# Top-2 expert weights and dispatch: one queue, 16 transfers, loads of 6, 28 and 31 rows ahead of a first store of 17

## The chip, the core and the metric

The kernel runs on one core of a Trainium2 chip. The metric is device microseconds for one execution, the median over several runs. VectorE (DVE) and ScalarE (ACT) compute, SyncE (SP) and ACT issue DMA transfers, and 16 DMA engines move the data between DRAM and the core's memory of 128 partitions.

## The reference

`x` has 16 x 1024 tokens of 512 floats, `router_logits` 8 floats for each token, and k is 2. Each token is written twice, scaled by the two largest of its softmax probabilities, brought to a sum of one; the smaller comes first.

```python
probs = np.exp(router_logits - logits_max)
probs = probs / np.sum(probs, axis=-1, keepdims=True)
topk_indices = np.argsort(probs, axis=-1)[..., -k:]
topk_probs = np.take_along_axis(probs, topk_indices, axis=-1)
topk_probs = topk_probs / np.sum(topk_probs, axis=-1, keepdims=True)
x_expanded = x[:, :, np.newaxis, :].repeat(k, axis=2)
return (x_expanded * topk_probs[..., np.newaxis]).astype(np.float32)
```

So 33.6 MB of tokens and 0.5 MB of logits are read and 67.1 MB written. With the two largest logits a difference d apart, the weights are the sigmoids of -d and d.

## The kernel before

The 16,384 tokens are 128 "rows" of 128 tokens: partition p holds a run of neighbouring tokens, and a row is one token of each partition, 2 KB a partition in and 4 KB out. The rows are cut into two groups of 65 and 63 (`GROUPS`). Within a group each partition's tokens lie next to each other in DRAM, so a transfer of n rows has one piece of n x 2 KB (a load) or n x 4 KB (a store) for each of 128 partitions, eight to each of the 16 DMA engines.

`xs` holds one group of tokens (65 rows). `osp` holds 16 rows of output. Some outputs are written into `osp`, others over tokens in `xs` that have been used up (`over`, line 98).

A group goes so. First its loads are issued on SP (line 112), group 0 in pieces of 2, 4, 2, 8, 17 and 32 rows, group 1 in pieces of 16, 16 and 31 (`LOADS`, line 51). Behind the first 6 rows of group 0 the logits are loaded in two transfers (lines 116 and 117), and `top2_weights` computes all weights for both groups into `WA`: eleven small VectorE operations on pairwise maxima and minima (lines 27 to 40), then two sigmoids on ACT (lines 42 and 43).

Then `plan` (line 121) is gone through: one VectorE product (line 128) and one store (line 136) for each entry. Its rows are 2 and 14 into `osp`, 16 over `xs`, 8 and 8 into the halves of `osp`, and the rest over `xs` (9 and 8 rows in group 0, 15 in group 1, `LAST`). The store of 2 rows is issued from ACT's queue, all others from SP's, in program order. In all there are 24 transfers: 9 loads of tokens, 2 of logits, 13 stores.

What orders the work are semaphores that the framework sets: a product waits for its tokens, and for the earlier store out of the buffer that it writes; a store waits for its product; the loads of group 1 wait for the stores out of the part of `xs` that they fill. Each transfer uses one of eight DMA semaphores in turn, and one that uses a semaphore again waits for the transfer that used it before.

Of the kernel before, what the change touches and what calls it, by code (L numbers as in the profile page):

```python
# [1 line left out]

# [4 lines left out]

F32 = mybir.dt.float32
ALU = mybir.AluOpType
ACTF = mybir.ActivationFunctionType  # L10
P = 128


def top2_weights(nc, pool, logits, M, E, tag=""):

    hi, lo, n = None, None, E  # L20
    while n > 1:
        n //= 2
        if hi is None:
            a, b = logits[:, :, 0:n], logits[:, :, n : 2 * n]
            nhi = pool.tile([P, M, n], F32, tag=f"hi{n}{tag}")
            nlo = b
            nc.vector.tensor_tensor(nhi, a, b, op=ALU.max)  # L27
            nc.vector.tensor_tensor(nlo, a, b, op=ALU.min)  # L28
        else:
            a, b = hi[:, :, 0:n], hi[:, :, n : 2 * n]  # L30
            nhi = pool.tile([P, M, n], F32, tag=f"hi{n}{tag}")
            nlo = pool.tile([P, M, n], F32, tag=f"lo{n}{tag}")
            tmp = pool.tile([P, M, n], F32, tag=f"tmp{n}{tag}")
            nc.vector.tensor_tensor(tmp, lo[:, :, 0:n], lo[:, :, n : 2 * n], op=ALU.max)  # L34
            nc.vector.tensor_tensor(nlo, a, b, op=ALU.min)  # L35
            nc.vector.tensor_tensor(nlo, nlo, tmp, op=ALU.max)  # L36
            nc.vector.tensor_tensor(nhi, a, b, op=ALU.max)  # L37
        hi, lo = nhi, nlo
    dlt = pool.tile([P, M], F32, tag=f"dlt{tag}")
    nc.vector.tensor_tensor(dlt, hi[:, :, 0], lo[:, :, 0], op=ALU.subtract)  # L40
    WA = pool.tile([P, M, 2], F32, tag=f"WA{tag}")
    nc.scalar.activation(WA[:, :, 0], dlt, ACTF.Sigmoid, scale=-1.0)  # L42
    nc.scalar.activation(WA[:, :, 1], dlt, ACTF.Sigmoid, scale=1.0)  # L43
    return WA

GROUPS = [65, 63]

LOADS = [[2, 4, 2, 8, 17, 32], [16, 16, 31]]


LAST = [[(48, 9), (57, 8)], [(48, 15)]]


@with_exitstack
def kernel(
    ctx: ExitStack,
    tc: tile.TileContext,  # L60
    x: bass.AP,
    router_logits: bass.AP,
    k: bass.AP,
    out: bass.AP,
):
    nc = tc.nc
    B, S, D = x.shape
    E = router_logits.shape[-1]
    N = B * S
    assert int(k) == 2 and E == 8 and N == P * sum(GROUPS)  # L70
    M = N // P

    L = 16
    x_v, o_v, rl_v = [], [], []
    t0 = 0
    for n in GROUPS:
        t1 = t0 + P * n
        x_v.append(
            x.rearrange("b s d -> (b s) d")[t0:t1].rearrange("(p m) d -> p m d", p=P)
        )  # L80
        o_v.append(
            out.rearrange("b s k d -> (b s) k d")[t0:t1].rearrange(
                "(p m) k d -> p m k d", p=P
            )
        )
        rl_v.append(
            router_logits.rearrange("b s e -> (b s) e")[t0:t1].rearrange(
                "(p m) e -> p m e", p=P
            )
        )  # L90
        t0 = t1

    wpool = ctx.enter_context(tc.tile_pool(name="wpool", bufs=1))
    logits = wpool.tile([P, M, E], F32)
    xs = wpool.tile([P, max(GROUPS), D], F32)
    osp = wpool.tile([P, L, 2, D], F32)

    def over(r, n, G):

        a = 2 * r - G
        return xs[:, a : a + 2 * n, :].rearrange("p (r k) d -> p r k d", k=2)

    h = L // 2
    e = 2
    m0 = 0
    for g, G in enumerate(GROUPS):
        r = 0  # L110
        for n in LOADS[g]:
            nc.sync.dma_start(xs[:, r : r + n, :], x_v[g][:, r : r + n, :])  # L112
            r += n
            if g == 0 and r == 6:

                nc.sync.dma_start(logits[:, :G], rl_v[0])  # L116
                nc.sync.dma_start(logits[:, G:], rl_v[1])
                WA = top2_weights(nc, wpool, logits, M, E)
        assert r == G
        begin = [(0, e, osp[:, :e]), (e, L - e, osp[:, e:])]  # L120
        plan = begin + [
            (L, L, over(L, L, 2 * L)),
            (2 * L, h, osp[:, :h]),
            (2 * L + h, h, osp[:, h:]),
        ]
        plan += [(r, n, over(r, n, G)) for r, n in LAST[g]]
        for r, n, og in plan:
            nc.vector.tensor_tensor(  # L128
                og,
                xs[:, r : r + n, :].unsqueeze(2).to_broadcast([P, n, 2, D]),  # L130
                WA[:, m0 + r : m0 + r + n, :].unsqueeze(3).to_broadcast([P, n, 2, D]),
                op=ALU.mult,
            )

            queue = nc.scalar if n == e else nc.sync
            queue.dma_start(o_v[g][:, r : r + n], og)
        m0 += G


# [1 line left out]
_INS = ['x', 'router_logits', 'k']  # L141
_OUTS = [((16, 1024, 2, 512), 'float32')]

_NUMBERS = {'k': 2}


# [26 lines left out]
```

## Time and profile before

| | |
|---|---|
| median of the runs | 240.22 us (240.09 to 240.84) |
| span of the profiled execution | 239.1 us |
| VectorE busy | 142.1 us (59%), 24 instructions |
| ScalarE busy | 1.8 us (1%), 3 instructions |
| DMA packets | 3456, of which 24 x 128 carry data and 24 x 16 write semaphores |
| moved | 101.19 MB, mean 423 GB/s over the span |
| share of the 16 DMA engines | SP's queue (q1) 96.5%, ACT's queue (q10) 2.1% |

The profiled execution has its own time, the span, from its first to its last instruction; the runs are other executions and include what lies around it. Times in the profile's rows are microseconds from the start of the span. L128 is line 128 of the kernel; SPq and ACTq are the engines' queues that issue DMA. A DMA packet counts for the stretch in which it starts, with the whole of its time, so shares of a short stretch can pass 100%.

### The profile page before, as it was taken

The page shows a single profiled execution, that of the slowest core. Times are in us where ns is not written, and L with a number is a line of the kernel's source. Part 1 is how long each engine was busy: PE and PEld are TensorE (multiplying, and loading weights), DVE is VectorE, ACT ScalarE, POOL GpSimd, SP SyncE. Part 2 cuts the span into 40 slices and gives each one's busy share as a digit, 9 for nine tenths or more (in the row PEclk, how much of TensorE's full clock was granted, in tenths as well). Part 3 has the DMA queues.
Part 4 walks back from the last instruction along what each step waited for, and adds up shares of the span by engine and source line. Part 5 has one row for each costly group of instructions (what it writes and reads, how often), then busy time and mean ns, then how long its engine had stood idle before and what let it go on. Part 6 is the DMA issues. An engine that isn't in the chain of part 4 may idle for free.

```text
span 239.1 us, 118 instructions
## 1 busy us (share of the span) xinstructions
DVE 142.1 (59%) x24; ACT 1.8 (1%) x3; POOL 0.2 (0%) x4
## 2 busy tenths in 40 slices
DVE  0589999900299699900000699999006999990000
ACT  2000000000000000000000000000000000000000
POOL 0000000000000000000000000000000000000000
DMA  7999989899999999999999999899899898999894
GB/s 254 440 463 426 441 388 526 329 460 460 417 438 406 400 422 438 438 481 396 433 438 438 438 511 396 384 502 394 384 460 515 362 493 367 428 433 486 380 483 175
DMA packets 3456, 101.19 MB, mean 423 GB/s; under 512 B 384, under 2 KB 512, under 8 KB 896
## 3 DMA queue, kind: packets, MB, share of 16 engines
q1 hardware_dynamic: 3168, 99.09, 96.5%
q10 hardware_dynamic: 288, 2.10, 2.1%
HBM read 34.08 MB, written 67.11 MB: 423 GB/s over the span
## 4 chain that ended last, share of the span: by engine, by line
DMA 52%; DVE 33%; issue 4%; SPq 1%; ACT 0%; DVEq 0%
DMA out_dram<-xs 24%; DVE xs L128 18%; DVE osp L128 13%; DMA out_dram<-osp 13%; DMA xs<-in_x_dram 13%; DMA logits<-in_router_logits_dram 3%; SPq L112 0%; DVE nhi L27 0%; DVE logits L28 0%; DVE nlo L36 0%; DVE nhi L37 0%; DVE nlo L35 0%; DVE tmp L34 0%; SPq L116 0%; ACT WA L42 0%
## 5 line engine op out<-in xcount | busy, mean ns | idle before, releaser
L128 DVE TENSOR_TENSOR osp<-xs,WA 128x8192 f32<-128x8192 f32 (+2 forms) x8 | 69.2, 8688 | 62.3 <-DMA xs<-in_x_dram 31.2
L128 DVE TENSOR_TENSOR xs<-xs,WA 128x16384 f32<-128x16384 f32 (+3 forms) x5 | 69.1, 13811 | 2.2 <-DMA out_dram<-xs 2.0
L27 DVE TENSOR_TENSOR nhi<-logits 128x512 f32<-128x512 f32 x1 | 0.7, 691 | 8.5 <-DMA logits<-in_router_logits_dram 8.5
L42 ACT ACT_TABLE_LOAD x1 | 1.3, 1283 | 0.7 <-PEq L154 0.7
L28 DVE TENSOR_TENSOR logits<-logits 128x512 f32<-128x512 f32 x1 | 0.7, 691 | 0.0
L35 DVE TENSOR_TENSOR nlo<-nhi 128x256 f32<-128x256 f32 (+1 forms) x2 | 0.7, 351 | 0.0
L37 DVE TENSOR_TENSOR nhi<-nhi 128x256 f32<-128x256 f32 (+1 forms) x2 | 0.7, 351 | 0.0
L36 DVE TENSOR_TENSOR nlo<-nlo,tmp 128x256 f32<-128x256 f32 (+1 forms) x2 | 0.7, 350 | 0.0
L34 DVE TENSOR_TENSOR tmp<-logits 128x256 f32<-128x256 f32 x1 | 0.4, 417 | 0.0
L42 ACT ACTIVATE WA<-dlt 128x128 f32<-128x128 f32 x1 | 0.3, 315 | 10.4 <-DVE dlt L40 10.4
L40 DVE TENSOR_TENSOR dlt<-nhi,nlo 128x128 f32<-128x128 f32 x1 | 0.3, 291 | 0.0
L43 ACT ACTIVATE WA<-dlt 128x128 f32<-128x128 f32 x1 | 0.3, 298 | 0.0
L34 DVE TENSOR_TENSOR tmp<-nlo 128x128 f32<-128x128 f32 x1 | 0.3, 283 | 0.0
L154 POOL MEMSET const-bfloat16-1.0<- 128x1 bf16 x1 | 0.1, 101 | 0.0
L154 POOL MEMSET const-uint8-127<- 128x1 uint8 x1 | 0.1, 101 | 0.0
L154 POOL MEMSET const-float32-0.0<- 128x1 f32 x1 | 0.1, 98 | 0.2 <-issue 0.2
L154 POOL MEMSET const-float32-1.0<- 128x1 f32 x1 | 0.1, 98 | 0.0
## 6 DMA issues: line engine op xcount, KB each, us to landing
out_dram<-osp SPq DMA_DIRECT2D x4, 4096.0 KB, 20.7
out_dram<-osp SPq DMA_DIRECT2D x2, 7168.0 KB, 32.4
xs<-in_x_dram SPq DMA_DIRECT2D x2, 4096.0 KB, 30.4
xs<-in_x_dram SPq DMA_DIRECT2D x1, 7936.0 KB, 40.9
out_dram<-xs SPq DMA_DIRECT2D x1, 7680.0 KB, 23.1
out_dram<-xs SPq DMA_DIRECT2D x1, 4608.0 KB, 20.4
xs<-in_x_dram SPq DMA_DIRECT2D x1, 4352.0 KB, 22.8
out_dram<-xs SPq DMA_DIRECT2D x1, 4096.0 KB, 21.4
```

The costliest lines, as they stand in the source:

```text
L27: nc.vector.tensor_tensor(nhi, a, b, op=ALU.max)
L28: nc.vector.tensor_tensor(nlo, a, b, op=ALU.min)
L34: nc.vector.tensor_tensor(tmp, lo[:, :, 0:n], lo[:, :, n : 2 * n], op=ALU.max)
L35: nc.vector.tensor_tensor(nlo, a, b, op=ALU.min)
L36: nc.vector.tensor_tensor(nlo, nlo, tmp, op=ALU.max)
L37: nc.vector.tensor_tensor(nhi, a, b, op=ALU.max)
L40: nc.vector.tensor_tensor(dlt, hi[:, :, 0], lo[:, :, 0], op=ALU.subtract)
L42: nc.scalar.activation(WA[:, :, 0], dlt, ACTF.Sigmoid, scale=-1.0)
L43: nc.scalar.activation(WA[:, :, 1], dlt, ACTF.Sigmoid, scale=1.0)
L128: nc.vector.tensor_tensor(og, xs[:, r : r + n, :].unsqueeze(2).to_broadcast([P, n, 2, D]), WA[:, m0 + r : m0 + r + n, :].unsqueeze(3).to_b ...
L154: nc = _bacc.Bacc("TRN2", target_bir_lowering=False, num_devices=1)
```

## The change

- Group 0 is loaded in 6, 28 and 31 rows instead of six pieces. The logits still stand behind the first 6 rows.
- Each group has four stores: 17, 16, 16, 16 rows in group 0, and 16, 16, 16, 15 in group 1 (`STORES`). The first and third come out of `osp`, the second and fourth over `xs`. All are issued from SP, so ACT's queue issues none. In all there are 16 transfers: 6 loads of tokens, 2 of logits, 8 stores.
- `osp` has 18 rows instead of 16. The logits and the scratch of `top2_weights` lie in its last three rows (15 to 17) until the weights are done; they had buffers of their own.
- The last two rows of group 0's first store, and the last four of each third store, are computed by ACT: two `Copy` activations of 512 elements for each row, with the weight as scale. VectorE computes the other 15 and 12. Everything else remains with VectorE.
- The store of 17 rows has 69,632 B a partition, and is built as 128 x 2 pieces of 34,816 B.

The diff, cut to its core:

```diff
-LOADS = [[2, 4, 2, 8, 17, 32], [16, 16, 31]]
-LAST = [[(48, 9), (57, 8)], [(48, 15)]]
+LOADS = [[6, 28, 31], [16, 16, 31]]
+STORES = [
+    [
+        (17, ("osp", 0), 2, "SP"),
+        (16, ("x", 1), 0, "SP"),
+        (16, ("osp", 0), 4, "SP"),
+        (16, ("x", 33), 0, "SP"),
+    ],
+    [
+        (16, ("osp", 0), 0, "SP"),
+        (16, ("x", 0), 0, "SP"),
+        (16, ("osp", 0), 4, "SP"),
+        (15, ("x", 33), 0, "SP"),
+    ],
+]
+OSP = 18
...
+    osp = pool.tile([P, OSP, 2, D], F32)
+    WA = pool.tile([P, M, 2], F32)
+    logits = osp[:, OSP - 1].rearrange("p k d -> p (k d)").rearrange("p (m e) -> p m e", e=E)
+    scratch = osp[:, OSP - 3 : OSP - 1].rearrange("p r k d -> p (r k d)")
...
+        for n, (home, a), by_act, queue in STORES[g]:
+            if home == "x":
+                og = xs[:, a : a + 2 * n, :].rearrange("p (r k) d -> p r k d", k=2)
+            else:
+                og = osp[:, a : a + n]
+            v = n - by_act
+            w = WA[:, m0 + r : m0 + r + n, :]
+            if v:
+                nc.vector.tensor_tensor(
+                    og[:, :v],
+                    xs[:, r : r + v, :].unsqueeze(2).to_broadcast([P, v, 2, D]),
+                    w[:, :v].unsqueeze(3).to_broadcast([P, v, 2, D]),
+                    op=ALU.mult,
+                )
+            for i in range(v, n):
+                for c in range(2):
+                    nc.scalar.activation(
+                        og[:, i, c], xs[:, r + i, :], ACTF.Copy, scale=w[:, i, c : c + 1]
+                    )
+            {"SP": nc.sync, "ACT": nc.scalar}[queue].dma_start(o_v[g][:, r : r + n], og)
+            r += n
```

`top2_weights` does the same eleven VectorE operations and two sigmoids on the same shapes; it takes its intermediate buffers out of `scratch`.

More of the change, by code (lines that the diff above doesn't have):

```diff
@@ L11 @@
 P = 128
-def top2_weights(nc, pool, logits, M, E, tag=""):
-    hi, lo, n = None, None, E
+E = 8
+D = 512
+GROUPS = [65, 63]
+M = sum(GROUPS)
+LOADS = [[6, 28, 31], [16, 16, 31]]
[13 more added lines that the diff above has]
+]
@@ L21, in top2_weights, with cut @@
+OSP = 18
+def top2_weights(nc, scratch, logits, WA):
+    used = [0]
+    def cut(n):
+        a = scratch[:, used[0] : used[0] + M * n].rearrange("p (m n) -> p m n", n=n)
+        used[0] += M * n
+        return a
+    a, b = logits[:, :, 0:4], logits[:, :, 4:8]
+    hi = cut(4)
+    lo = b
+    nc.vector.tensor_tensor(hi, a, b, op=ALU.max)
+    nc.vector.tensor_tensor(lo, a, b, op=ALU.min)
+    n = 4
     while n > 1:
         n //= 2
[L23 to L37, printed above, removed]
@@ L38, in top2_weights @@
-        hi, lo = nhi, nlo
[L39 to L49, printed above, removed]
-LOADS = [[2, 4, 2, 8, 17, 32], [16, 16, 31]]
-LAST = [[(48, 9), (57, 8)], [(48, 15)]]
+        a, b = hi[:, :, 0:n], hi[:, :, n : 2 * n]
@@ new lines, in top2_weights @@
+        nhi, nlo, tmp = cut(n), cut(n), cut(n)
+        nc.vector.tensor_tensor(tmp, lo[:, :, 0:n], lo[:, :, n : 2 * n], op=ALU.max)
+        nc.vector.tensor_tensor(nlo, a, b, op=ALU.min)
+        nc.vector.tensor_tensor(nlo, nlo, tmp, op=ALU.max)
+        nc.vector.tensor_tensor(nhi, a, b, op=ALU.max)
+        hi, lo = nhi, nlo
+    dlt = cut(1)
+    nc.vector.tensor_tensor(dlt, hi, lo, op=ALU.subtract)
+    nc.scalar.activation(WA[:, :, 0], dlt[:, :, 0], ACTF.Sigmoid, scale=-1.0)
+    nc.scalar.activation(WA[:, :, 1], dlt[:, :, 0], ACTF.Sigmoid, scale=1.0)
@@ L66 @@
     nc = tc.nc
[L67 to L73, printed above, removed]
+    N = x.shape[0] * x.shape[1]
+    assert int(k) == 2 and router_logits.shape[-1] == E and x.shape[2] == D
+    assert N == P * M
+    xf = x.rearrange("b s d -> (b s) d")
+    of = out.rearrange("b s k d -> (b s) k d")
+    rf = router_logits.rearrange("b s e -> (b s) e")
     x_v, o_v, rl_v = [], [], []
@@ L77, with load_logits @@
         t1 = t0 + P * n
[L78 to L90, printed above, removed]
-        t0 = t1
[L93 to L107, printed above, removed]
+        x_v.append(xf[t0:t1].rearrange("(p m) d -> p m d", p=P))
+        o_v.append(of[t0:t1].rearrange("(p m) k d -> p m k d", p=P))
+        rl_v.append(rf[t0:t1].rearrange("(p m) e -> p m e", p=P))
+        t0 = t1
+    pool = ctx.enter_context(tc.tile_pool(name="pool", bufs=1))
+    xs = pool.tile([P, max(GROUPS), D], F32)
+    osp = pool.tile([P, OSP, 2, D], F32)
+    WA = pool.tile([P, M, 2], F32)
+    logits = osp[:, OSP - 1].rearrange("p k d -> p (k d)").rearrange("p (m e) -> p m e", e=E)
+    scratch = osp[:, OSP - 3 : OSP - 1].rearrange("p r k d -> p (r k d)")
+    def load_logits():
+        nc.sync.dma_start(logits[:, : GROUPS[0]], rl_v[0])
+        nc.sync.dma_start(logits[:, GROUPS[0] :], rl_v[1])
     m0 = 0
@@ L112 @@
             nc.sync.dma_start(xs[:, r : r + n, :], x_v[g][:, r : r + n, :])
+            if g == 0 and r < 6 <= r + n:
+                load_logits()
+                top2_weights(nc, scratch, logits, WA)
             r += n
[L114 to L118, printed above, removed]
         assert r == G
[L120 to L136, printed above, removed]
+        r = 0
+        for n, (home, a), by_act, queue in STORES[g]:
[19 more added lines that the diff above has]
+            r += n
+        assert r == G
         m0 += G
```

## The prediction

> **What bounds the kernel now.** I read the page first: span, busy engines, share of the DMA engines, queues, and the time to landing of the last store.
>
> ```profile
> span 239.1 us, 118 instructions
> DVE 142.1 (59%) x24; ACT 1.8 (1%) x3; POOL 0.2 (0%) x4
> ...
> DMA  7999989899999999999999999899899898999894
> DMA packets 3456, 101.19 MB, mean 423 GB/s; under 512 B 384, under 2 KB 512, under 8 KB 896
> q1 hardware_dynamic: 3168, 99.09, 96.5%
> q10 hardware_dynamic: 288, 2.10, 2.1%
> ...
> out_dram<-xs SPq DMA_DIRECT2D x1, 7680.0 KB, 23.1
> ```
>
> VectorE works 59% of the span, the 16 DMA engines 96.5 + 2.1 = 98.6% of it, in every slice but the first and the last. Then I asked by stretch where the missing 1.4% lies, and the timeline for the first issue and the last.
>
> ```profile
> 0.00:1.74 1.74, 0.00 (x0) 1.01 (x1) 0.20 (x4) 1.00 0.00 0
> 164.00:236.00 72.00, 37.41 (x4) 0.00 (x0) 0.00 (x0) 1.00 1.00 432
> ...
> 0.73 0.86 SPq L112 DMA_DIRECT2D xs<-in_x_dram  x2
> 215.19 0.33 SPq L136 DMA_DIRECT2D out_dram<-xs  x1
> ```
>
> In a row by stretch the last two columns are DMA share and GB/s. Nothing moves before 1.74; the share is 1.00 while the last four stores drain, though VectorE works only 37.41 of those 72 us. The last store lands 23.1 us after its issue at 215.19, at 238.3. So the time is 1.74 us of start, then the length of an unbroken DMA queue, then some 0.8 us of ending. Idle VectorE time costs nothing, and an edit counts only if it changes what a DMA engine spends on a packet, or opens a hole in the queue. The profiled execution spans 239.1 us and the median of the runs is 240.2; I carry differences from one to the other unchanged.
>
> **What a packet costs.** The DMA view of a narrow stretch counts packets, MB and share, and share times length times 16, divided by packets, is the time of one packet. Here are the answers for 47.2 to 62 us, 63.9 to 80, and 84 to 91.5.
>
> ```profile
> q1 hardware_dynamic: 112, 6.42, 100.1%
> ...
> q1 hardware_dynamic: 98, 6.36, 91.1%
> ...
> q1 hardware_dynamic: 97, 3.18, 98.1%
> ```
>
> The first holds 14-row store packets (57,344 B): 14.8 x 1.001 x 16 / 112 = 2.116 us. The second holds 97 packets of 65,536 B and a semaphore write: 16.1 x 0.911 x 16 / 97 = 2.419 us. The third holds 32,768 B packets: 7.5 x 0.981 x 16 / 97 = 1.214 us. Two of the last make one of the second plus 0.008 us, so a packet costs about 0.008 us of its own and the rest is bytes.
>
> **Fewer, larger transfers.** Before there are 24 transfers of 128 packets, 24 x 8 = 192 packets on each engine. After there are 16, and the store of 17 rows, 69,632 B a partition, is built as two pieces each, so 17 x 8 = 136 packets. The bytes are the same. Saved: 56 x 0.008 = 0.45 us, on the path, because the queue is the path. The first load goes from 2 + 4 rows to 6 in one; its bytes ahead of the logits are the same, and 8 packets fewer is 0.06 us, counted already.
>
> The Trainium skill says otherwise: "DMA: Bandwidth & Descriptors", section "Anatomy of one DMA", fits 2.0 us of fixed cost to each transfer beside its bytes. By it, an estimate, eight transfers fewer would take off 16 us; the share of 1.00 at 432 GB/s in the row from 164 to 236 disagrees, for no engine idles between transfers there.
>
> **The store beside the loads.** ACT's queue (q10) carries 2 rows in each group beside SP's loads. Its issue, then the stretches from 15.3 to 18.78 and from 18.78 to 20.7:
>
> ```profile
> 15.32 0.38 ACTq L136 DMA_DIRECT2D out_dram<-osp  x1
> ...
> q1 hardware_dynamic: 38, 1.32, 88.3%
> ...
> q1 hardware_dynamic: 23, 0.80, 96.9%
> q10 hardware_dynamic: 20, 0.16, 20.2%
> ```
>
> Beside q10 the loads' 34,816 B packets take 1.92 x 0.969 x 16 / 23 = 1.293 us. Scaled from the 1.214 us row by bytes they would take 0.008 + 1.206 x 34,816 / 32,768 = 1.289. So taking the store away from the loads frees under 0.005 us for each packet, nothing I can count.
>
> **From load to store.** Two stretches hold exactly the last packet of each engine ahead of a group's first large store, 43.2 to 43.9 us (16 packets of 65,536 B) and 160.4 to 161.5 (16 of 63,488 B).
>
> ```profile
> q1 hardware_dynamic: 16, 1.05, 433.8%
> ...
> q1 hardware_dynamic: 16, 1.02, 224.1%
> ```
>
> They took 0.7 x 4.338 = 3.04 us and 1.1 x 2.241 = 2.47 us, where 2.419 and 2.343 are usual: 0.62 us lost in group 0, 0.12 in group 1. Group 1's change keeps its 31-row load and a large store behind it, so 0.12 stays. In group 0 the load of 32 rows becomes one of 31, like group 1's, so the loss may stay at 0.62 or fall to 0.12, and with a hole at the seam to zero: 0 to -0.6 us. The nearest row in size is group 1's, but I can't say size is the cause; I take -0.25.
>
> **The slowest engine.** The 16 semaphore writes of the last store, in 236.5 to 237.2, 237.2 to 237.8 and 237.8 to 238.2:
>
> ```profile
> q1 hardware_dynamic: 14, 0.00, 1.1%
> ...
> q1 hardware_dynamic: 1, 0.00, 0.1%
> q1 hardware_dynamic: 1, 0.00, 0.1%
> ```
>
> One engine of 16 finishes over 0.6 us behind 14 of the others, and it sets the end. That is an accident of this execution as far as the trace tells. Another chain of larger packets may have a better or worse one, between -0.7 and +0.3 us; I take -0.2.
>
> **The seam of group 0, where the change takes its risk.** Before, the first large store is ready long ahead of the queue's need. After, its 15 VectorE rows need the load of 28 rows. The rows, the first of them the DMA packets from 8.0 to 8.53 us:
>
> ```profile
> DMA packets 52, 0.21 MB, mean 402 GB/s; under 512 B 0, under 2 KB 0, under 8 KB 52
> ...
> 8.53 0.69 DVE L27 TENSOR_TENSOR nhi<-logits 128x512 f32<-128x512 f32 x1 [8.53 <-DMA logits<-in_router_logits_dram]
> ...
> L128 DVE TENSOR_TENSOR xs<-xs,WA 128x16384 f32<-128x16384 f32 x2 | 34.4, 17224 | 0.1
> L128 DVE TENSOR_TENSOR osp<-xs,WA 128x14336 f32<-128x14336 f32 x2 | 30.2, 15084 | 0.0
> L128 DVE TENSOR_TENSOR xs<-xs,WA 128x15360 f32<-128x15360 f32 x1 | 16.2, 16158 | 0.0
> ...
> L128 DVE TENSOR_TENSOR osp<-xs,WA 128x8192 f32<-128x8192 f32 x4 | 34.6, 8688 | 30.6 <-DMA out_dram<-osp 30.6
> L42 ACT ACTIVATE WA<-dlt 128x128 f32<-128x128 f32 x1 | 0.3, 315 | 10.4 <-DVE dlt L40 10.4
> ```
>
> VectorE sees the logits at 8.53, after it 8.47. The 28 rows follow: 8 x 2.116 = 16.93, seen at 25.40. The product of 15 rows takes 16.16: 41.56. SP then issues the store. The load of 31 rows takes 8 x 2.343 = 18.74 more and would be seen at 44.14. By the rows at 43.2 and 43.9 plus 3.04 us the engines of before went on to the store between 46.2 and 46.9, spread over 0.7 us; and a landing is seen some 0.5 us after the last engine's data (no packet under 2 KB, so none of the logits' and no semaphore write of theirs, after 8.0). So after the change they run dry from 42.9 to 43.6.
>
> How long from issue to first packet? The first load's row says 0.73 to 1.74, 1.0 us, into empty engines. ACT's says 15.32 to 18.78, 3.5 us, into engines full with another queue's packets. By the first the store starts at 42.6, ahead of the dry point by 0.3 to 1.0 us. By the second it starts at 45.0, and 1.4 to 2.1 us are lost. I take the first, because at the seam no other queue holds packets in front; allowing for the last engines to be served, +0.1 us. The Trainium skill, same page, section "Queues, rings and completion order", has each DMA engine take turns between queues by whole packets; by that, 3.5 us would be mostly a wait for a turn, which one queue alone doesn't have. No run here shows it yet.
>
> **The rest of the chain has room.** ACT's two rows are four activations of 512 elements; at most 4 x 0.315 = 1.26 us each, 5.0 us, beside VectorE's 16.16. Group 0's second store: VectorE 41.56 + 17.22 = 58.8, while the queue is busy with 17 rows to about 43.3 + 8 x 2 x 1.289 = 63.9. Third: the wait for that store's landing ends near 64.5, 12 rows take 12.95 (between the rows of 8,192 and 14,336 elements) to 77.5, ACT's four rows at most 8 x 1.26 = 10.1 us beside it; the queue needs it at 63.9 + 19.35 = 83.3. Fourth: 94.7 against 102.6. Group 1: loads run from about 122 to 160; VectorE has the first 16 rows near 132.5 and the product at 149.7 against 160. Third: 180.3 + 12.95 = 193.3 against 198.8. The least of these margins is 5 us, so a product given up to ACT or a shared buffer costs nothing there; if the cover failed, only what exceeds 5 us would show. SP's queue is in order, and no load stands behind a store that comes late: the loads of group 1 are issued after 94.7 and needed at 122. The two logits loads and the scratch in `osp` add no wait, since rows 15 and 16 of the first store are written by ACT behind its own sigmoids.
>
> **Sum.** -0.45 - 0.25 - 0.2 + 0.1 = -0.8 us: 238.3 us of span, 239.4 us as a median.
>
> **Rivals.** A measurement of this kernel can tell about 0.3%, 0.72 us: faster is below 239.5, slower above 240.94.
>
> *Only the packets count.* The switch from load to store costs 0.6 again and a straggler of the same size appears: -0.45 + 0.1, 239.9 us, no change that can be told. For it: two of my four terms are accidents of one execution. Chance 0.30.
>
> *The hole at the seam.* The store of 17 rows starts as ACT's row had it, 3.5 us from issue. It decides once issue to first packet passes about 1.6 us, or VectorE is late by 0.6 us. At 3.5 us the hole is 1.75 on average: -0.45 - 0.2 + 1.75 = +1.1, 241.3 us. Against it: the row of the first load, and that issue still comes a microsecond before the dry point. Chance 0.20, of which 0.03 with a small hole ends within 0.3%.
>
> *A fixed cost for each transfer after all.* By a mechanism that the share of 1.00 would have to hide, eight transfers would give 16 us, 224 us. Chance 0.01; the page named above is its only source.
>
> *The change doesn't do what it says.* The two pieces per partition of the 17-row store fall unevenly on the engines: if some engine had twice 20.6 us, 20 us more, 260 us. Nothing in the trace has such a shape; all that it has run evenly. Chance 0.02.
>
> The forecast itself has 0.47. Faster: 0.47 + 0.01 = 0.48. Within 0.3%: 0.30 + 0.03 = 0.33. Slower: 0.17 + 0.02 = 0.19. The forecast's own range is 238.6 (switch and straggler both gone) to 239.5. The range for 8 in 10 reaches up through the first rival and most of the hole, 238.6 to 241.2.
>
> **What would show it.** Right: the DMA share near 1.00 from 2 to 236 with q10 gone, 136 data packets an engine, the first packet of the 17-row store about 1 us after SP's issue near 41.6. Wrong: a stretch near 43 us with a low share; VectorE's product of 15 rows starting after 25.4 or lasting over 16.2 us; a last load packet again near 3.0 us; the last semaphore write no earlier than 237.8.

## The result, and the profile after

The changed kernel takes 242.22 us (241.44 to 242.77, 6 runs) against 240.16 (240.02 to 240.84, 6 runs) for the kernel before: 1.008 times, interval 1.0068 to 1.0092. It is slower, by 2.06 us. The forecast was 239.4, range 238.6 to 241.2.

The page of the changed kernel, the lines that answer to those of before:

```profile
span 240.4 us, 125 instructions
DVE 131.0 (54%) x19; ACT 14.4 (6%) x23; POOL 0.2 (0%) x4
...
DMA  7997998899998989898969999998989999999894
DMA packets 2432, 101.19 MB, mean 421 GB/s; under 512 B 256, under 2 KB 384, under 8 KB 512
q1 hardware_dynamic: 2432, 101.19, 98.3%
```

The same bytes go in 2432 packets instead of 3456, and the DMA engines are busy for 98.3% of a longer span, against 98.6% before. So no large hole stands in the queue. Packets take longer, and the engines end further apart.

The queue turns three times: from group 0's loads to its stores, from these to group 1's loads, and from those to group 1's stores. I call these the first, second and third turn, and what a packet takes there beyond its usual time the loss. The next fence has the DMA view of the changed kernel for stretches that hold just the 16 packets around each turn. The columns are packets, MB and share. In order: 40.53 to 41.03 us (last load packets before the first turn), 119.1 to 119.85 (last store packets before the second), 122.4 to 123.2 (first load packets behind it, with 16 semaphore writes of 0.01 us), 158.2 to 160.35 (last load packets before the third).

```profile
q1 hardware_dynamic: 16, 1.02, 468.6%
...
q1 hardware_dynamic: 16, 1.05, 422.2%
...
q1 hardware_dynamic: 32, 0.52, 178.3%
...
q1 hardware_dynamic: 16, 1.02, 144.7%
```

Worked out as in the prediction, a packet at the first turn takes 0.5 x 4.686 = 2.34 us, the usual time. At the second it takes 0.75 x 4.222 = 3.17 where 2.42 is usual, behind it 0.8 x 1.783 - 0.01 = 1.42 where 1.21 is, and at the third 2.15 x 1.447 = 3.11 where 2.34 is. So each engine loses nothing at the first turn, 0.75 + 0.20 at the second and 0.77 at the third. Before, the first cost 0.62 and the third 0.12. The second cost nothing there: its last store packets, from 121.1 to 122.1 us in the kernel before, took 1.0 x 1.213 = 1.21 us, the usual time for 32,768 B.

```profile
q1 hardware_dynamic: 16, 0.52, 121.3%
```

The four stores between the first two turns also run a little long. From 82.81 to 100.45 us, 128 packets of 65,536 B and 16 semaphore writes:

```profile
q1 hardware_dynamic: 144, 8.39, 110.2%
```

That is 17.64 x 1.102 x 16 / 128 = 2.430 us a packet against 2.419, 0.08 us a transfer. By the packet records of the trace the four stores of group 0 lose 0.23 together.

Last, the semaphore writes of the last store, from 237.3 to 238.6 and from 238.6 to 239.4:

```profile
q1 hardware_dynamic: 15, 0.00, 0.6%
...
q1 hardware_dynamic: 1, 0.00, 0.1%
```

The engines end scattered over two microseconds, one far behind.

**Which execution the profile of before showed.** With every run's span beside its time, the two differ by about 1.8 us in both kernels: 242.22 and 240.4 after, 240.16 and 238.4 before. The profiled execution of before had a span of 239.1, so it was the run of 240.84, the slowest of the first three, and not a typical one. Typical executions lie 2.0 us apart in span, not 1.3.

### The profile page after: what moved, and what is told of

The parts are those of the page before. It is cut to its first block, busy times and chain, and to the rows that moved or that the text cites. A ratio compares the mean times of both kernels' runs of the same rounds, so it can differ in the third digit from the quotient of the medians.

```text
span 240.4 us, 125 instructions
## 1 busy us (share of the span) xinstructions
DVE 131.0 (54%) x19; ACT 14.4 (6%) x23; POOL 0.2 (0%) x4
## 2 busy tenths in 40 slices
DMA packets 2432, 101.19 MB, mean 421 GB/s; under 512 B 256, under 2 KB 384, under 8 KB 512
## 3 DMA queue, kind: packets, MB, share of 16 engines
q1 hardware_dynamic: 2432, 101.19, 98.3%
## 4 chain that ended last, share of the span: by engine, by line
DMA 48%; DVE 39%; SPq 1%; issue 0%; DVEq 0%
DMA xs<-in_x_dram 26%; DVE osp L126 25%; DMA out_dram<-osp 23%; DVE xs L126 14%; SPq L105 0%; SPq L104 0%; SPq L111 0%; SPq L137 0%; DVEq L126 0%
## 5 line engine op out<-in xcount | busy, mean ns | idle before, releaser
L126 DVE TENSOR_TENSOR osp<-xs,WA 128x12288 f32<-128x12288 f32 (+2 forms) x4 | 59.3, 14825 | 72.6 <-DMA xs<-in_x_dram 52.4
L126 DVE TENSOR_TENSOR xs<-xs,WA 128x16384 f32<-128x16384 f32 (+1 forms) x4 | 67.8, 16958 | 0.3
L134 ACT ACTIVATE osp<-xs,WA 128x512 f32<-128x512 f32 x20 | 12.6, 708 | 162.8 <-DMA out_dram<-osp 150.3
L52 DVE TENSOR_TENSOR osp<-osp 128x512 f32<-128x512 f32 x1 | 0.7, 693 | 8.2 <-DMA osp<-in_router_logits_dram 8.2
L66 ACT ACTIVATE WA<-osp 128x128 f32<-128x128 f32 x1 | 0.3, 315 | 10.2 <-DVE osp L65 10.2
L53 DVE TENSOR_TENSOR osp<-osp 128x512 f32<-128x512 f32 x1 | 0.7, 692 | 0.0
L60 DVE TENSOR_TENSOR osp<-osp 128x256 f32<-128x256 f32 (+1 forms) x2 | 0.7, 352 | 0.0
L62 DVE TENSOR_TENSOR osp<-osp 128x256 f32<-128x256 f32 (+1 forms) x2 | 0.7, 352 | 0.0
L61 DVE TENSOR_TENSOR osp<-osp 128x256 f32<-128x256 f32 (+1 forms) x2 | 0.7, 352 | 0.0
L59 DVE TENSOR_TENSOR osp<-osp 128x256 f32<-128x256 f32 (+1 forms) x2 | 0.7, 351 | 0.0
L67 ACT ACTIVATE WA<-osp 128x128 f32<-128x128 f32 x1 | 0.3, 297 | 0.0
## 6 DMA issues: line engine op xcount, KB each, us to landing
xs<-in_x_dram SPq DMA_DIRECT2D x2, 7936.0 KB, 40.6
```

The lines of the kernel that those rows point to most:

```text
L52: nc.vector.tensor_tensor(hi, a, b, op=ALU.max)
L53: nc.vector.tensor_tensor(lo, a, b, op=ALU.min)
L66: nc.scalar.activation(WA[:, :, 0], dlt[:, :, 0], ACTF.Sigmoid, scale=-1.0)
L67: nc.scalar.activation(WA[:, :, 1], dlt[:, :, 0], ACTF.Sigmoid, scale=1.0)
L126: nc.vector.tensor_tensor(og[:, :v], xs[:, r : r + v, :].unsqueeze(2).to_broadcast([P, v, 2, D]), w[:, :v].unsqueeze(3).to_broadcast([P, v ...
L134: nc.scalar.activation(og[:, i, c], xs[:, r + i, :], ACTF.Copy, scale=w[:, i, c : c + 1])
```

## The experiments

Four theories came up, one after the other. Theory 1: a packet before a turn takes longer when one of 65,536 B stands beside the turn. Theory 2: a turn always costs, by how the engines stand to each other. Theory 3, after the first four runs: a first turn that is covered, with its store issued early, costs something once and makes the later ones free, and the change's seam (its first turn) misses that. Theory 4, its rival: where the buffers lie. Below, the dry point is the moment when the engines run out of group 0's load packets, 42.9 us for the first of them in the changed kernel, and the lead of a store is how long before that it is issued.

**Smaller packets at the turns.** Twice in the changed kernel:

```diff
 a1: -(16, ("x", 33), 0, "SP")     +(8, ("x", 33), 0, "SP"), (8, ("x", 49), 0, "SP")
     -(16, ("osp", 0), 0, "SP")    +(8, ("osp", 0), 0, "SP"), (8, ("osp", 8), 0, "SP")
 a2: -(16, ("x", 33), 0, "SP")     +(1, ("x", 33), 0, "SP"), (15, ("x", 35), 0, "SP")
     -(16, ("osp", 0), 0, "SP")    +(14, ("osp", 0), 0, "SP"), (2, ("osp", 14), 0, "SP")
```

> The changed kernel with the last store of group 0 cut into 8 + 8 rows and the first store of group 1 cut into 8 + 8, so packets of 32,768 B stand on the store side of the second and third turn of the queue. Theory 1 (the last packet of each engine before a turn is stretched when a packet of 65,536 B stands on either side): the stretch before the second turn falls from 0.75 us to under 0.1, that of the first packets behind it from 0.21 to under 0.1, and the one before the third turn from 0.77 to under 0.15; two transfers more cost 0.13 us; span 240.4 - 1.5 = 238.9, time about 240.7 us. Theory 2 (the stretch comes with a turn whatever the sizes, and its size is set by how the engines stand to each other): all three stay within 0.3 us of what they were, span 240.4, time 242.2 us. Both: the time outside the span stays at 1.8 us, since ACT issues no transfer here either.

> The changed kernel with the last store of group 0 cut into 1 + 15 rows (packets of 61,440 B before the second turn) and the first store of group 1 into 14 + 2 (packets of 57,344 B behind the third, as in the kernel before). Theory 1a (it takes a packet of exactly 65,536 B): both stretches fall to 0.15 us or less, span about 239.1. Theory 1b (it grows with the size): second turn about 0.7 us, third about 0.7 us, span 240.4. Theory 2: no change beyond 0.3 us at each turn.

Measured: 242.18 us (1.0072, 1.0053 to 1.009) and 241.97 (1.0075, 1.0057 to 1.0094). The DMA view of a1 before the second turn, 120.3 to 121.3 us, and before the third, 158.3 to 160.05:

```profile
q1 hardware_dynamic: 16, 0.52, 201.4%
...
q1 hardware_dynamic: 16, 1.02, 169.5%
```

Packets of 32,768 B take 2.01 us where 1.21 is usual, a loss of 0.80 as with packets twice the size. At the third turn 2.97, a loss of 0.62. In a2 the losses are 0.59 and 0.95. Theory 1 falls: no loss went below 0.15 us. Theory 2 had these numbers about right, but it is too simple: a1's second turn moves the very rows that the kernel before moves there, where it loses nothing.

**ACT's queue, in both directions.** The last store of the changed kernel from ACT's queue, and the kernel before without ACT's queue:

```diff
 a3: -(15, ("x", 33), 0, "SP")                        +(15, ("x", 33), 0, "ACT")
 b1: -queue = nc.scalar if n == e else nc.sync        +queue = nc.sync
```

> The changed kernel with the very last store issued from ACT's queue instead of SP's. Inside the span theories 1 and 2 both expect 240.4 within 0.3 us: the turns stand as they were, and the last store drains beside the one before it. For the 0.76 us by which the time outside the span grew (1.06 before, 1.82 after): if it hangs on ACT's queue carrying no transfer, it falls back to about 1.1 us here and the time is about 241.5; if it hangs on the 20 activations or anything else in the change, it stays at 1.8 and the time is 242.2.

> The kernel before with its two stores of 2 rows issued from SP's queue like the others, so that no store runs beside loads. The prediction's reading: no difference inside the span beyond 0.2 us. Theory 2 in the form that stores beside the loads keep the engines out of step: the stretch before the third turn rises from 0.12 to 0.6 us or more. Theory 1: the packet behind both turns is one of 8,192 B, the packet before them 65,536 B in the first and 63,488 B in the third; first turn 0.3 to 0.6 us, third under 0.15. Outside the span: 1.8 us if it hangs on ACT's queue, 1.1 if not.

Measured: a3 241.71 us (1.0059, 1.0041 to 1.0078), b1 240.26 (1.0006, 0.9995 to 1.0016). In a3 the second turn loses 0.63 and 0.21 behind it, the third 1.03. The 1.8 us outside the span is there in all four, so the question about it rested on the untypical execution of before. That no store runs beside loads costs and brings nothing by itself: b1's first turn, from 40.65 to 41.3 us, takes 3.12 where 2.42 is usual, a loss of 0.70, its third, from 158.15 to 158.9, 2.42 where 2.34 is, and its engines end together, all 16 semaphore writes between 236.6 and 237.5:

```profile
q1 hardware_dynamic: 16, 1.05, 480.0%
...
q1 hardware_dynamic: 16, 1.02, 322.1%
...
q1 hardware_dynamic: 16, 0.00, 1.0%
```

**The seam covered, the buffers moved, the two pieces gone.**

```diff
 c1: -LOADS = [[6, 28, 31], [16, 16, 31]]     +LOADS = [[6, 11, 17, 31], [16, 16, 31]]
 c2: +pad = pool.tile([P, 1024], F32)         (ahead of xs)
     +nc.gpsimd.memset(pad[:, 0:1], 0.0)
 c3: before: logits = wpool.tile(...) moved behind osp
 c4: -(17, ("osp", 0), 2, "SP")               +(16, ("osp", 0), 2, "SP"), (1, ("osp", 16), 0, "SP")
```

> The changed kernel with group 0 loaded in 6, 11, 17 and 31 rows, so that the first store of 17 rows is ready some 12 us ahead of the first turn instead of 1.5. Theory 3 (the engines' places to each other: the stretch at a first turn that is covered puts the engines into an order in which later turns are free, and the seam of the change, run nearly dry, skips that): 0.6 us stretch at the first turn, then under 0.15 at the second and third, and no stretch in the stores between; span about 238.5. Theory 4 (where the buffers lie): about 0.6 us more at the first turn, second and third stay near 0.75 (with 0.25 behind the second) and 0.75, span about 241.

> The changed kernel with a buffer of 4,096 B a partition put ahead of xs, which puts xs where it lay in the kernel before (the logits' buffer stood there). Theory 4: second and third turn fall under 0.15 us, stores between 43 and 123 us lose their 0.2 us of stretch, span about 238.7. Theory 3: nothing changes, span 240.2 to 240.7.

> The kernel before with its logits buffer allocated behind osp, so that xs starts at the bottom as in the changed kernel. Theory 4: second and third turn rise to 0.6 us or more, time 241.5 us or more. Theory 3: no change, 240.2 us.

> The changed kernel with the store of 17 rows made as 16 and 1, so that no partition's run is cut into two pieces of 34,816 B; the seam is 1.1 us earlier. If the two pieces throw the engines out of order, the stores between 43 and 123 us lose their stretch, and second and third turn fall to 0.15 us or less: span about 238.6. Theories 3 and 4: second and third turn stay at 0.6 us or more each, span 240.2 to 240.8.

Measured: c1 240.39 us (1.0003, 0.9993 to 1.0012), c2 241.88 (1.0071, 1.005 to 1.0091), c3 240.23 (0.9994, 0.9981 to 1.0006), c4 241.19 (1.0032, 1.0018 to 1.0047). Theory 4 falls with c2 and c3 as the cause of the loss. c2's second turn loses 0.52, with 0.48 behind it, and its third 0.29; its span of 239.9 us lies under what theory 3 had, so whether the place of the buffers moves part of the loss stays open. c3's turns lose 0.38, 0 and 0.22. c1 gives back all that the change lost. Its DMA view, 40.6 to 41.1 us (before the first turn), 120 to 120.55 (second), 158.1 to 159 (third), and the last semaphore writes, 236.5 to 237.5:

```profile
q1 hardware_dynamic: 16, 1.02, 690.7%
...
q1 hardware_dynamic: 16, 1.05, 439.6%
...
q1 hardware_dynamic: 16, 1.02, 263.3%
...
q1 hardware_dynamic: 16, 0.00, 0.9%
```

A packet at the first turn takes 3.45 us where 2.34 is usual and loses 1.11, more than the 0.6 expected. The second is free (2.418), the third nearly (2.37), and the engines end together. c4 came out in between, as no theory had it: its store is issued a microsecond earlier than in the changed kernel, and its turns lose 0.32, 0.27 and 0.71. Its ten runs lie spread from 240.14 to 241.90 us, from c1's time nearly to the changed kernel's. It removed the stretch of the stores between, but two pieces are not the cause, since c1 has them and no stretch either.

c4's trace also shows the first two turns engine by engine, since each packet begins within some 5 ns of the end of the one before it on its engine, and so each engine's packets can be followed. The ten engines that lost 0.29 us or more at the first turn lost at most 0.17 at the second, and the four that lost nothing at the first lost 0.57 to 0.98 there. The third turn is not freed in this way: it cost every engine 0.31 us or more, also those that had paid.

**The lead alone.** c1 also changed the pieces of the loads. d1, e3 and d2 leave them as they are and move only the issue of the first store, by the rows that ACT takes:

```diff
 d1: -(17, ("osp", 0), 2, "SP")     +(17, ("osp", 0), 6, "SP")
 e3: -(17, ("osp", 0), 2, "SP")     +(17, ("osp", 0), 4, "SP")
 d2: -(17, ("osp", 0), 2, "SP")     +(17, ("osp", 0), 0, "SP")
```

> The changed kernel, loads as they are, with six instead of two of the first store's 17 rows given to ACT, so that VectorE's product has 11 rows and the store is issued near 36.9 us, some 6 us ahead of the dry point instead of 1.5. If the early issue is what counts (theory 3), and not that the loads come in more pieces: 0.4 to 1.1 us of stretch at the first turn, under 0.15 at the second and third, no stretch in the stores between, time about 240.4 us. If the pieces of the loads did it: no change, first turn 0, second 0.75 and more, third about 0.75, time 242.2.

> The changed kernel with four rows of the first store on ACT: VectorE's product 14.0 us, store issued near 39.3, 3.6 us ahead of the dry point. Leads so far: 1.5 us, turns of 0, 1.0 and 0.77; 2.6 us (with 16 and 1 rows), 0.32, 0.27 and 0.71; 5.8 us, 1.11, 0.03 and 0.05. If the lead has to exceed what one packet of the last load takes, 2.34 us, plus a start of about 1 us: first turn near 1.1, second and third under 0.15, time 240.4. If it takes two packets, 4.7 us and a start: in between as at 2.6 us, time 241.2.

> The changed kernel with all 17 rows of the first store on VectorE: product 18.3 us, store issued near 43.5, so that the engines stand empty for 1.0 to 1.7 us. Theory 3: first turn without stretch, second and third stretched as in the changed kernel, about 1.7 us together; the hole comes on top, span 241.5 to 242.2, time 243.3 to 244.0. A rival, that a near miss at the seam does the harm and a clean hole resets the engines: second and third under 0.15, time about 242.0 us.

Measured: d1 240.49 us (1.0012, 1.0003 to 1.0021), e3 240.41 (1.001, 1.0000 to 1.0019), d2 242.43 (1.0094, 1.0077 to 1.0111). The issue in e3's timeline, and its last load packets before the first turn, from 40.55 to 41.2 us:

```profile
39.43 0.40 SPq L137 DMA_DIRECT2D out_dram<-osp  x1
...
q1 hardware_dynamic: 16, 1.02, 520.6%
```

They take 0.65 x 5.206 = 3.38 us, a loss of 1.04, and the second and third turn lose 0.00 and 0.04. d1, issued at 37.12, loses 1.11, 0.00 and 0.05. The lines for e3's second turn (120.0 to 120.57 us) and its third (158.15 to 158.75):

```profile
q1 hardware_dynamic: 16, 1.05, 424.2%
...
q1 hardware_dynamic: 16, 1.02, 397.7%
```

Two microseconds of lead, got from two rows more on ACT, are all that lies between the changed kernel's 242.22 us and 240.41. c1 moves the lead by the loads and leaves ACT's rows alone, d1 and e3 do the opposite, and all three come out the same.

In d2 the store comes too late: its issue, the DMA packets from 43.3 to 44.35 us, then from 44.35 to 44.51, and the last packets before the second turn (120.75 to 120.95) and the third (159.7 to 160.1):

```profile
43.44 0.40 SPq L137 DMA_DIRECT2D out_dram<-osp  x1
...
q1 hardware_dynamic: 1, 0.00, 0.1%
...
q1 hardware_dynamic: 16, 0.56, 808.6%
...
q1 hardware_dynamic: 16, 1.05, 1601.6%
...
q1 hardware_dynamic: 16, 1.02, 787.8%
```

Nothing but a semaphore write for a microsecond, then all engines start within 0.16 us, 0.9 us after the issue. Second and third turn lose 0.79 and 0.81. So a hole doesn't reset anything, and theory 3 stands. I had expected 243.3 or more. The hole of about 1.3 us cost only 0.2 beside the changed kernel: d2's engines, which start together, also end together (all between 238.7 and 239.6), and in its trace no engine lags behind the rest.

**What the first turn costs.** c1 with the last load packets smaller, and with a store on ACT's queue beside the loads as before:

```diff
 d3: +LOADS = [[6, 11, 17, 27, 4], [16, 16, 31]]
 d4: +LOADS = [[6, 11, 17, 16, 15], [16, 16, 31]]
 e1: c1 with (17, ("osp", 0), 2, "SP") -> (2, ("osp", 0), 0, "ACT"), (15, ("osp", 2), 2, "SP")
 e2: e1 with (16, ("osp", 0), 0, "SP") -> (2, ("osp", 0), 0, "ACT"), (14, ("osp", 2), 0, "SP")
```

> The kernel with the covered seam (group 0 in 6, 11, 17 and 31 rows: first turn 1.11 us, time 240.39) with its 31 rows cut into 27 and 4, so that the last packets before the first turn have 8,192 B. If the stretch at a covered first turn grows with the packet before it: under 0.5 us, second and third stay under 0.15, time about 239.8. If it is a fixed price of that turn: 0.6 to 1.1 us, time 240.4.

> The kernel with the covered seam with its 31 rows cut into 16 and 15, last packets of 30,720 B. By size: first turn 0.4 to 0.7 us, time about 240.1. Fixed price: 0.6 to 1.1 us, time 240.4. Theory 3 for both: second and third turn under 0.15 us.

> The kernel with the covered seam (loads of 6, 11, 17, 31), with group 0's first store as in the kernel before: 2 rows issued from ACT beside the loads, then 15 from SP (two of them computed by ACT; no two-piece store, 16 other transfers, 136 packets an engine). In the kernels whose ACT queue carries a store beside group 0's loads the first turn cost 0.62 and 0.38 us, in those without 0.70 to 1.11. If the store beside the loads is what makes the turn cheaper: first turn 0.4 to 0.6 us, second and third under 0.25, time 239.7 us, a little under the kernel before. If not: first turn 0.7 to 1.1, time 240.3.

> The same, with 2 rows from ACT's queue ahead of 14 in group 1 too. If a store beside the loads always softens the turn behind it: third turn 0 to 0.1 us, time 239.7. If it unsettles an order that was there (third turn 0.12 and 0.22 us in the kernels before with it, 0.03 to 0.08 in those without): third turn 0.1 to 0.25, time 239.9.

Measured: d3 240.48 us (1.0013, 1.0002 to 1.0025), d4 240.35 (1.0006, 0.9991 to 1.0022), e1 240.15 (0.9995, 0.9986 to 1.0003), e2 240.23 (1.0000, 0.9991 to 1.0009). Size isn't it: d3's load of 4 rows loses 1.09 us in all, with packets an eighth as large, and d4's last load 0.82. d3's third turn loses 0.27, where I had expected less than 0.15; its trace is of its slowest run, 241.00 us. With ACT's store e1 loses 0.60 and e2 0.49 at the turn, but their loads beside that store lose 0.15 and 0.28 more, so the two together come to about 0.75. e1 is the best of the changed design, and ties with the kernel before; neither e1 nor e2 reached the 239.7 us that a cheaper first turn was to bring.

One table has the kernels that differ in lead; the losses are microseconds for each engine, worked out from each trace as above. The lead is the issue of group 0's first large store ahead of 42.9 us, where the changed kernel's first engine runs dry; for the kernel before, ahead of 46.2 us, where its own engines get to the store. The others side with their leads: a1, a2, a3 and c2, as late as the changed kernel, lose nothing at the first turn and 1.3 to 1.9 behind it, and b1, c3, d3, d4, e1 and e2, all early, lose 0.38 to 1.09 at the first and at most 0.27 at a later one.

| kernel | lead, us | first turn | second, and behind it | third | time, us |
|---|---|---|---|---|---|
| d2 | -0.5 | 0 and a hole | 0.79, 0.16 | 0.81 | 242.43 |
| changed | 1.5 | 0 | 0.75, 0.20 | 0.77 | 242.22 |
| c4 | 2.6 | 0.32 | 0.27, 0.01 | 0.71 | 241.19 |
| e3 | 3.5 | 1.04 | 0, 0 | 0.04 | 240.41 |
| d1 | 5.8 | 1.11 | 0, 0 | 0.05 | 240.49 |
| c1 | 11.7 | 1.11 | 0, 0 | 0.03 | 240.39 |
| before | 16 | 0.62 | 0, 0 | 0.12 | 240.16 |

## Why the prediction was wrong

**The packets: right.** 19 x 128 packets and semaphore writes are left, a full packet takes 2.42 us in group 1's stores as before, and 56 x 0.008 = 0.45 us of the queue is gone. The 2.0 us for each transfer, which the prediction took from the Trainium skill ("DMA: Bandwidth & Descriptors", "Anatomy of one DMA"), is measured there for a transfer issued from GpSimd. It is no price in this queue: c1, with 17 transfers, takes 1.0003 times as long as the kernel before with 24.

**The seam: right in its times, wrong in what it decides.** The timeline of the changed kernel:

```profile
25.19 16.16 DVE L126 TENSOR_TENSOR osp<-xs,WA 128x15360 f32<-128x15360 f32 x1 [13.06 <-DMA xs<-in_x_dram]
41.44 0.40 SPq L137 DMA_DIRECT2D out_dram<-osp  x1
41.45 17.23 DVE L126 TENSOR_TENSOR xs<-xs,WA 128x16384 f32<-128x16384 f32 x1
58.71 0.35 SPq L137 DMA_DIRECT2D out_dram<-xs  x1
64.50 12.96 DVE L126 TENSOR_TENSOR osp<-xs,WA 128x12288 f32<-128x12288 f32 x1 [5.82 <-DMA out_dram<-osp]
```

25.19, 41.44, 58.71 and 64.50 stand against 25.40, 41.56, 58.8 and 64.5 forecast. The first store packets start at 42.94 us, where the first engine runs dry, and the hole over all engines is below 0.1 us, as taken. Issue to first packet is 0.9 us in d2's empty engines, near the row that I took and not ACT's 3.5. The rival with the hole, which held most of my chance of slower, didn't happen. (Its price of +1.1 left out the -0.6 at the first turn that I had myself given to a hole; with it the sum is +0.5.) What I missed is that a seam just short of a hole takes the loss from the first turn and puts more of it on the next two.

**From load to store: the step that failed.** I counted 0.62 us at the first turn as something local that could stay, shrink or vanish, and took -0.25. It vanished, -0.62. But I wrote of the third turn that its 0.12 "stays", because its load kept its size, and I had no term for the second at all, since nothing showed there. The third went to 0.77, the second to 0.75 + 0.20, and the stores between lost 0.23: +1.83 us in place of 0. So the step that failed is the overlap at the turns: I took each turn's loss as its own, and they hang together. d1 and e3 show it by the lead alone: with the first store known early an engine pays 1.04 to 1.11 us at the first turn and at most 0.05 at each later one, in the mean of the 16. c4 shows for the second turn that it is the engines that paid which are free there; for the third turn such a link is not shown.

**The slowest engine: wrong, and the link to the median with it.** I counted -0.2 on a straggler of the profiled execution and carried the sum over to the median. A typical execution of before has a span 0.7 us shorter, about what the straggler lags, and the traces of b1 and c3, which are of typical length, have none; so the median had nothing to lose there. After the change there is one, and it ended past the 237.8 us that the prediction named as a sign of being wrong. By the packet records it is the engine that lost most at the second turn and behind it, where the losses fall unevenly. Against b1, which has the same transfers as before and a typical span, 238.5, the account, in microseconds and roughly, is: packets -0.45, first turn -0.70, stores +0.23, second turn +0.95, third +0.70, some 0.3 in small gaps and the start, in all +1.0 for the mean engine, as its last packets end at 237.99 instead of 236.98 by the packet records. The last engine adds +0.9: it ends 1.3 us behind the mean instead of 0.4. Together 1.9, the difference of the spans.

**The rest: right.** Beside the product of 15 rows ACT needs 2.6 us for its two rows, and the 12-row products take 12.96 us as interpolated; no cover failed. The store beside the loads was worth nothing, as b1 shows at 1.0006.

## What to carry to other kernels

When the DMA queue is the bound, cutting a load-to-store seam as fine as the queue allows can cost more than it saves: here a store issued 3.5 us ahead of the end of the loads gave 240.41 us, and one issued 1.5 us ahead 242.22, with no hole in either. A loss at one place of a queue shouldn't be dropped from a sum, or a free place counted as free, before it is seen what the one has to do with the other; a covered variant of the change, with its first store ready early like c1's, would have told. And before differences are carried from a profiled execution to a median, its time should be looked up among the runs.

## What the runs showed of the hardware

With the first store issued 3.5 us or more ahead of the dry point, the first change from loads to stores cost each engine 0.4 to 1.1 us in its last load packets, and the next two changes cost 0.0 to 0.3. Issued 1.5 us ahead or later, the first cost nothing and the next two, with the packets behind the second, 1.7 to 1.9 us between them in the kernel as changed, in a1, a2, a3 and in d2, and 1.3 in c2.

The lead at which it tips lies between 1.5 and 3.5 us, with c4's 2.6 in between. That is near the start of the last load packets, which begin at 40.5 to 41.2 us. By an estimate with d2's 0.9 us from issue to first packet, the store of e3 is there at 40.3, just ahead of them, that of c4 at 41.2, just after the last of them has begun (40.98 in c4), that of the changed kernel at 42.3, late in them. That it is this moment which decides is not shown, as no run moves the last load packets against the store's issue near the tipping lead. "DMA: Bandwidth & Descriptors" of the Trainium skill, section "Two DMAs through the same engine are not ordered", says that the descriptors of a queue start in order but are pipelined, with reading and writing sides apart; that fits a store that begins to be read while the last load packet is still written. No run here shows that it is so, nor why one such turn frees the later ones, nor why c4's third turn stays dear. It also stays open why the covered first turn costs 0.38 to 0.70 us in the kernels with the old pieces (before, b1, c3) and 1.1 in c1, d1 and e3; neither the size of the last load packet (d3, d4) nor ACT's store alone (b1, without it, 0.70) explains it.
